# Where the splits of the output weights stand: program order for the gate's and the output's, old states through GpSimd's queue, the samples' last step ranked first

## The chip, the core and the metric

The kernel runs on one core of a Trainium2 chip. The metric is the device time of one execution in microseconds (us), and less is better. Engines are named as in the profile: PE is TensorE (matmuls), DVE is VectorE, ACT is ScalarE, POOL is GpSimd, SP is SyncE, which here only issues transfers. Each engine takes its instructions in the order in which the program stands for it, so an instruction that waits holds up all that stand behind it on its engine.

## The reference

One inference step of a two-layer decoder for 256 prompt positions and 8 sample tokens, handled together as 264 columns. Each layer is half a SwiGLU, a mixer, half a SwiGLU. The mixer of layer 0 is RWKV-7 time mixing, the one of layer 1 a retention.

```python
def step(S, inp):
    r_t, d_t, k_t, v_t, kk_t, a_t = inp
    sa = jnp.einsum('bhvk,bhk->bhv', S, -kk_t)
    S = (S * d_t[:, :, None, :] + sa[..., None] * (kk_t * a_t)[:, :, None, :]
         + v_t[..., None] * k_t[:, :, None, :])
    return S, jnp.einsum('bhvk,bhk->bhv', S, r_t)
...
y = (_head_norm(y, RW_GN_EPS) * lnx_g + lnx_b)
y = y + jnp.sum(r_h * k_h * r_k, axis=-1, keepdims=True) * v_h
out = (y.reshape(B, L, D) * g) @ wo
...
x = x + out
h = _rmsnorm(x, w['ln_ffn2'][i])
x = x + FFN_RES * _swiglu(h, w['ff2_wg'][i], w['ff2_wu'][i], w['ff2_wd'][i])
```

The gate is `g = sigmoid(xg @ g1) @ g2`. The prompt starts from a zero state; each sample has an old state `S` of its own, which is read for `sa` (`S` times the key), for the output row (`S` times decay and receptance) and for the new state that is written out.

## The kernel before

Activations lie transposed: 1024 features as 8 tiles of 128 partitions, 264 columns each (`self.x[:, m, :]`). Weights come as 364 units of 512 KB, each eight 128x128 blocks in the order in which the program uses them. `unit` (line 157) loads a unit into `raw` (three buffers) on SP's queue. `split` (line 163) makes two parts of it in a reduced float format: ACT copies `raw` to `hi`, DVE subtracts `hi` from `raw` to give `lo` (three buffers each). A product of full accuracy is then three matmuls (`mm3`, line 249): `hi` with the high part of the activation, `hi` with its low part, `lo` with its high part. Some weights (key, receptance, value) are not split; their matmuls read `raw` itself (`xv,raw` in the profile).

`rwkv` is written as Python generators: a main one, `stream`, and sides that are woven in (`weave`) by a model of the engines' clocks and by each side's rank. The tile framework then reorders each engine's instructions by a model of its own, except that an instruction handed to `keep_in_program_order` stays behind the one that was written before it on its engine. In `split` this pinning is off (`self.pinned = False`), so the framework may place the ACT copy and the DVE subtraction of a unit wherever its model thinks the unit has landed.

The end of the RWKV part, around the change, in the order of `stream`:

- the value products of the 8 tiles (`xv,raw`); meanwhile the heads, in four groups of two tiles (`heads2`), run many small matmuls on PE with evacuations on ACT and DVE between them. Names of one group: `KQ`, `bT`, `M` (M1), `aT`, `VK`, `z`, `WT`, `G`, `Y`, and `PI`, which POOL makes;
- the gate's second weight, one unit of 8 blocks (`rw_g2`), used at the end of each group;
- the output weight `rw_wo`, 8 units. Output tiles 0 to 3 take four units together, as the groups finish; tiles 4 to 7 take one unit each, 24 matmuls. When tile m is summed, DVE adds it to `x[:, m]`, and `feed(m)` (line 257) prepares the next norm from it: ACT makes `ah` (scaled copy) and the square (`ss` for tile 0, `sq` for the others), DVE makes `al` and adds the square to `ss`.

The samples' old states (`in_wkv`, 2 MB) are read twice here, four loads of 512 KB each time, into `dS` tiles that share three buffers with other tiles: `saved` forms `sa`, `decode_rows` the output rows; both use `states_with` (line 1033), where POOL multiplies a piece by a row and DVE sums it. `decode_rows` is the samples' last step; its rank among the sides is `decode` in the table `TU`, and a lower rank stands earlier.

Of the kernel before, what the change touches and what calls it, by code (L numbers as in the profile page):

```python
# [41 lines left out]
class Step:  # L42
    def __init__(self, ctx, nc, tc, io):
        self.ctx, self.nc, self.tc, self.io = ctx, nc, tc, io
        self.order, self.early = [], {}
        self.done = {}
        self.clock = dict(pe=0.0, dve=0.0, act=0.0, pool=0.0, dma=0.0)
        self.ready = {}
        self.now = self.start = 0.0
        self.table = None  # L50
        self.use(MODEL)
        self.pinned, self.pins = False, ()
        self.late = nc.gpsimd
        e = ctx.enter_context
        self.cp = e(tc.tile_pool(name="cp", bufs=1))
        self.raw_p = e(tc.tile_pool(name="raw", bufs=3))
        self.hi_p = e(tc.tile_pool(name="hi", bufs=3))
        self.lo_p = e(tc.tile_pool(name="lo", bufs=3))
        self.a_p = e(tc.tile_pool(name="a", bufs=18))
        self.w_p = e(tc.tile_pool(name="w", bufs=1))  # L60
        self.ps_p = e(tc.tile_pool(name="ps", bufs=8, space=PSUM))
# [101 lines left out]
    def split(self, raw, first=False):  # L163
        hi = self.hi_p.tile([128, UT, 128], F32R, tag="hi", name="hi")
        lo = self.lo_p.tile([128, UT, 128], F32R, tag="lo", name="lo")
        now, start, self.start = self.now, self.start, 0.0
        pinned, self.pinned = self.pinned, False
        for i, j in FIRST if first else ((0, UT),):
            s = slice(i, j)
            self.act(hi[:, s], raw[:, s])  # L170
            self.tt(lo[:, s], raw[:, s], hi[:, s], ALU.subtract)
        self.now, self.start, self.pinned = now, start, pinned
        if self.model["AHEAD"]:
            for t in (hi, lo):
                self.ready.pop(t.tensor.name, None)
        return hi, lo
# [268 lines left out]
class Rwkv(Step):  # L445
# [18 lines left out]
    def rwkv(self, gain):  # L464
        nc, tc, ps_, late = self.nc, self.tc, self.ps, self.late
# [5 lines left out]
        with ExitStack() as ctx:  # L471
# [68 lines left out]
            def stream():  # L540
                loras = [scaled("wa1", ((0, 64, 1), (64, 128, 4))), scaled("rw_g1", ((0, 128, 5),))]
                acc.extend((ps_(), ps_()) for _ in loras)
                rs = None
                for k0, k1 in ((0, TU["RK"]), (TU["RK"], KT)):
                    for (W0, W2), (Y0, Y2) in zip(loras, acc):
                        for k in range(k0, k1):
                            self.mm3(Y0[:, 0:T], W0[k], xg[k], k == 0, k == KT - 1)
                            self.mm3(Y2[:, 0:T + NS], W2[k], xt[k], k == 0, k == KT - 1)
                            yield
                    if rs is None:  # L550
                        rs = self.rms()

                        for f in range(KT):
                            nc.gpsimd.memset(hz[f][:, 0:1], 0.0)
                            self.stt(hz[f][:, 1:T + 1], self.x[:, f, :], par("ln_mix.0", f), rs)
                            self.tt(xx[f][:, 0:NP], hz[f][:, 0:NP], hz[f][:, 1:NP + 1], ALU.subtract)
                            self.tt(xx[f][:, NP:T], sh[:, f, :], hz[f][:, NP + 1:T + 1], ALU.subtract)
                            mixed("k", 2, f)
                            mark(f"mix{f}")
                            nc.gpsimd.tensor_copy(sho[:, f, :], hz[f][:, NP:T + 1])  # L560
                self.late.dma_start(self.io["sho"], sho)
                wa2.extend(self.wt("wa2", 0, f) for f in range(KT))
                for n, g in (("hidden", hidden(rs)), ("rates", rates()), ("mixr", mixes("r", 0)), ("mixv", mixes("v", 3))):
                    self.beside(TU[n], g)
                if TU["HE"]:
                    heads()
                for g in range(2):
                    kp = [ps_()[:, 0:T] for _ in range(4)]
                    for k in range(KT):
                        yield f"mix{k}"  # L570
                        for j in range(4):
                            prod(kp[j], "k", k, 4 * g + j)
                            yield
                    k_out(g, kp)
                self.beside(TU["inverse"], inverse())
                self.beside(TU["saved"], saved())
                def vs(f):
                    p = ps_()[:, 0:T]
                    for k in range(KT):
                        if f == 0 and "v" not in WHOLE:  # L580
                            yield f"vp{k}"
                        prod(p, "v", k, f)
                        yield
                    values(f, p)

                def rs_(f):
                    p = ps_()[:, 0:T]
                    for k in range(KT):
                        prod(p, "r", k, f)
                        yield  # L590
                    st[f]["rc"] = slot("rc")
                    self.act(st[f]["rc"], p)
                    self.act(dq[:, 4, f, :], p[:, NP:T])
                    mark(f"r{f}")
                    self.beside(TU["prep"], prep(f))

                for i in range(KT + TU["IL"]):
                    if i < KT:
                        yield from rs_(i)
                    if i == KT - 1 and not TU["HE"]:  # L600
                        heads()
                    if i >= TU["IL"]:
                        yield from vs(i - TU["IL"])
                g2.extend(self.wt("rw_g2", 0, f) for f in range(KT))

                po = {}

                def wo(m, k):
                    if k == 0:
                        po[m] = ps_()[:, 0:T]  # L610
                    self.mm3(po[m], self.wt("rw_wo", k, m), go[k], k == 0, k == KT - 1)

                n0, n1 = TU["n0"], TU["n1"]
                for k in range(KT - 1):
                    yield f"go{k}"
                    for m in range(n0):
                        wo(m, k)
                        yield
                for m in range(n0, n1):
                    for k in range(KT - 1):  # L620
                        wo(m, k)
                        yield
                yield f"go{KT - 1}"
                for m in range(KT):
                    for k in range(KT - 1 if m < n1 else 0, KT):
                        wo(m, k)
                        yield
                    self.tt(self.x[:, m, :], po[m], self.x[:, m, :], ALU.add)
                    self.feed(m, gain)

            wa2, g2 = [], []
            A3, AT = (P1.tile([128, 32, 32], F32, name=k) for k in ("A3", "AT"))
# [401 lines left out]
            def states_with(row, out):  # L1034

                def load(i):
                    if i * NV < 64:
                        Sd = by_value(big("dS"))
                        nc.sync.dma_start(Sd, by_value(self.io["wkv"][:, part_of(i)[1]]))
                        return Sd  # L1040

                for i in range(64 // NV):
                    vs = part_of(i)[0]
                    if i == 0:
                        ahead = load(0), load(1)
                        yield 2.5
                    Sd, ahead = ahead[0], (ahead[1], load(i + 2))
                    self.pool_tt(Sd, Sd, row.unsqueeze(1).to_broadcast([128, NV, 64]))
                    yield
                    self.vec("tensor_reduce", Sd, out=out[:, vs], op=ALU.add, axis=AX.X)  # L1050
                    yield
# [76 lines left out]
def by_value(t):  # L1128
    return t.rearrange("p (v k) -> p v k", v=NV)
# [5 lines left out]

NM = 60
NW = 10
TU = dict(PEF=1.0, DVEF=1.0, ACTF=1.5, LP=0.5, LD=0.12, LA=0.15, SLACK=0.2, AHEAD=1, wk='mm', wr='mm', wv='mm', IL=8, pin_stream=0, pin_hidden=1, pin_rates=0, pin_mixes=0, pin_lengths=0, pin_stage=0, pin_inverse=0, pin_prep=1, pin_head=0, pin_saved=0, vp='r7', hv=0, hw=1, hidden=8, rates=7, mixr=1, mixv=5, inverse=0, saved=4, prep=3, head=2, headf=0.01, decode=9, lengths=3, stage=7, by_step=0, HE=0, wait_r=None, wait_v='k0', PW=4, SW=8, RK=3, INVY=8, pre=3.5, n0=3, n1=4)
WHOLE = "krv"
SLOT = 266  # L1140

# [445 lines left out]
```

## Time and profile before

| what | value |
|---|---|
| time, median of 3 runs | 1299.81 us (1299.36 to 1302.5) |
| the profiled execution | 1302.37 us, of which the trace spans 1300.6 us |
| PE busy | 1258.5 us, 97% of the span |
| DVE busy | 866.2 us, 67% |
| ACT busy | 669.0 us, 51% |
| POOL busy | 87.1 us, 7% |
| chain that ended last | 90% PE |

The profiled execution took 2.56 us more than the median of the runs. PE is busy for nearly the whole span, so the time is PE's work plus the stretches in which it stands still or in which its granted clock is at the lower level (1.2 instead of 2.4 GHz, shown as 0.50).

### The profile page before, as it was taken

The numbers are of one execution on the slowest core, as the hardware profiler recorded it, in microseconds if no ns is written. First come the engines' busy times: TensorE is split into PE (matmuls) and PEld (weight loads), VectorE is DVE, ScalarE is ACT, GpSimd is POOL, SyncE is SP. The second block draws the span as 40 slices with busy tenths as digits, with TensorE's granted clock in tenths as the row PEclk, the third lists the DMA queues.
The fourth block names the chain that finished last, engine by engine and source line by source line (L and its number), as shares of the span: only waits on it lengthen the run. The fifth ranks groups of instructions, "written<-read, shape, count | busy, mean of one in ns | idle before, by whom it ended". The sixth has DMA issues, their size and how long they took to land.

```text
span 1300.6 us, 28601 instructions
## 1 busy us (share of the span) xinstructions
PE 1258.5 (97%) x11932; PEld 1187.7 (91%) x11932; DVE 866.2 (67%) x1400; ACT 669.0 (51%) x1162; POOL 87.1 (7%) x177
## 2 busy tenths in 40 slices
PE   9999999998788999999999999999999999999996
PEld 9999998677666899999999999988888799999996
DVE  6766567589355777765666665577878866666654
ACT  6544442652334577764455544455765554544542
POOL 0000001133330000000000000002111100000000
PEclk9999999999979999999999999999999999999998
DMA  7555554232420467665557655669879565555552
GB/s 231 186 185 182 179 162 144 91 124 89 148 84 4 153 200 225 221 198 179 178 178 260 197 184 180 203 237 327 301 286 333 204 196 181 176 184 182 182 178 82
DMA packets 67329, 241.16 MB, mean 185 GB/s; under 512 B 7568, under 2 KB 8976, under 8 KB 67072
## 3 DMA queue, kind: packets, MB, share of 16 engines
q1 hardware_dynamic: 60624, 216.82, 50.8%
q0 software_dynamic: 5968, 21.31, 4.3%
q8 instruction: 93, 1.52, 0.5%
q10 hardware_dynamic: 608, 1.21, 0.3%
q14 instruction: 36, 0.29, 0.1%
HBM read 216.95 MB, written 22.35 MB: 184 GB/s over the span
## 4 chain that ended last, share of the span: by engine, by line
PE 90%; DVE 5%; DMA 2%; ACT 2%; issue 1%; DVEq 0%; SPq 0%; ACTq 0%
PE ps L138 89%; DMA raw<-in_w 2%; DVE tm L105 1%; PE ps L153 1%; DVE V L105 1%; ACT hi L90 1%; DVE lo L105 1%; DMA S<-in_ret 0%; DVE KQ L105 0%; ACT L90 0%; DVE xf L105 0%; DVE A L132 0%; DVE on L120 0%; DVE rs L126 0%; ACT yl L90 0%
## 5 line engine op out<-in xcount | busy, mean ns | idle before, releaser
L90 ACT ACTIVATE hi<-raw 128x1024 fp32r<-128x1024 f32 (+1 forms) x344 | 362.7, 1055 | 447.8 <-PE ps L138 218.9
L105 DVE TENSOR_TENSOR lo<-raw,hi 128x1024 fp32r<-128x1024 f32 (+1 forms) x344 | 418.8, 1218 | 238.5 <-ACT hi L90 237.2
L138 PE MATMUL ps<-ah,hi 128*128 128x264 f32 (+1 forms) x1824 | 522.7, 289 | 0.9 <-ACT ah L90 0.9
L138 PE MATMUL ps<-al,hi 128*128 128x264 f32 (+1 forms) x1824 | 516.9, 285 | 0.0
L138 PE MATMUL ps<-ah,lo 128*128 128x264 f32 (+1 forms) x1824 | 514.5, 285 | 0.0
L138 PEld LDWEIGHTS ps<-ah,hi 128*128 128x128 f32 x1824 | 342.8, 189 | 9.0 <-issue 7.4
L138 PEld LDWEIGHTS ps<-al,hi 128*128 128x128 f32 x1824 | 343.5, 189 | 4.1 <-issue 2.9
L138 PEld LDWEIGHTS ps<-ah,lo 128*128 128x128 f32 x1824 | 342.4, 189 | 0.1
L138 PE MATMUL ps<-hh,hi 128*128 128x264 f32 x832 | 237.1, 285 | 0.0
L138 PE MATMUL ps<-hl,hi 128*128 128x264 f32 x832 | 237.0, 285 | 0.0
L138 PE MATMUL ps<-hh,lo 128*128 128x264 f32 x832 | 236.8, 285 | 0.0
L138 PEld LDWEIGHTS ps<-hl,hi 128*128 128x128 f32 x832 | 156.8, 188 | 0.0
L138 PEld LDWEIGHTS ps<-hh,lo 128*128 128x128 f32 x832 | 156.7, 188 | 0.0
L138 PEld LDWEIGHTS ps<-hh,hi 128*128 128x128 f32 x832 | 156.4, 188 | 0.1
L105 DVE TENSOR_TENSOR h<-s,ps 128x264 f32<-128x264 f32 x88 | 37.1, 428 | 49.0 <-PE ps L138 46.9
L105 DVE TENSOR_TENSOR t<-ps,rs 128x264 f32<-128x264 f32 x88 | 37.2, 431 | 19.2 <-PE ps L138 19.0
L114 DVE SCALAR_TENSOR_TENSOR S<-ps,ks,S 128x512 f32<-128x512 f32 x64 | 45.0, 745 | 5.9 <-PE ps L138 5.9
L90 ACT ACTIVATE S<-S 128x1024 f32<-128x1024 f32 x32 | 33.7, 1055 | 16.9 <-DMA S<-in_ret 16.5
L105 DVE TENSOR_TENSOR hl<-h,hh 128x264 fp32r<-128x264 f32 x88 | 37.0, 428 | 0.3
L90 ACT ACTIVATE hh<-h 128x264 fp32r<-128x264 f32 x88 | 35.3, 408 | 3.6 <-DVE h L105 3.6
L90 ACT ACTIVATE s<-t 128x264 f32<-128x264 f32 x88 | 35.3, 410 | 3.5 <-DVE t L105 3.5
L138 PE MATMUL ps<-part,hi 128*128 128x264 f32 (+1 forms) x176 | 34.5, 309 | 2.3 <-ACT part L90 2.3
(260 smaller groups left out, 1232.9 us busy)
## 6 DMA issues: line engine op xcount, KB each, us to landing
raw<-in_w SPq DMA_DIRECT2D x363, 512.0 KB, 3.5
S<-in_ret SPq DMA_DIRECT2D x32, 512.0 KB, 5.8
out_sret<-S POOLq DMA_DIRECT2D x32, 512.0 KB, 3.7
dS<-in_wkv SPq DMA_DIRECT2D x8, 512.0 KB, 4.0
Sd<-in_wkv SPq DMA_DIRECT2D x4, 512.0 KB, 5.2
out_swkv<-Sd POOLq DMA_DIRECT2D x4, 512.0 KB, 3.8
out_pret<-so POOLq DMA_DIRECT2D x8, 256.0 KB, 2.3
rcst<-in_rcst SPq DMA_DIRECT2D x1, 1100.0 KB, 6.4
```

The lines of the kernel that those rows point to most:

```text
L90: ins = self.nc.scalar.activation(out=out, in_=in_, func=func, scale=scale, **kw)
L105: ins = self.nc.vector.tensor_tensor(out=out, in0=a, in1=b, op=op)
L114: ins = self.nc.vector.scalar_tensor_tensor(out=out, in0=a, scalar=s, in1=b, op0=op0, op1=op1)
L138: ins = self.nc.tensor.matmul(out=out, lhsT=lhsT, rhs=rhs, start=start, stop=stop)
L153: self.nc.tensor.transpose(out, in_, ident)
```

## The change

Three edits. While `stream` is between the last value product and the last output tile, `in_order` is set, and the splits of units first used there keep their place in the program on ACT and DVE: that is the gate's unit and the 8 output units. The `dS` loads are issued by POOL instead of SP. The rank of the samples' last step goes from 9 to 1.

```diff
--- before.py
+++ after.py
@@ -50,6 +50,7 @@
         self.table = None
         self.use(MODEL)
         self.pinned, self.pins = False, ()
+        self.in_order = False
         self.late = nc.gpsimd
         e = ctx.enter_context
         self.cp = e(tc.tile_pool(name="cp", bufs=1))
@@ -164,10 +165,10 @@
         hi = self.hi_p.tile([128, UT, 128], F32R, tag="hi", name="hi")
         lo = self.lo_p.tile([128, UT, 128], F32R, tag="lo", name="lo")
         now, start, self.start = self.now, self.start, 0.0
-        pinned, self.pinned = self.pinned, False
+        pinned, self.pinned = self.pinned, self.in_order
         for i, j in FIRST if first else ((0, UT),):
             s = slice(i, j)
-            self.act(hi[:, s], raw[:, s])
+            self.pin(self.act(hi[:, s], raw[:, s]))
             self.tt(lo[:, s], raw[:, s], hi[:, s], ALU.subtract)
         self.now, self.start, self.pinned = now, start, pinned
         if self.model["AHEAD"]:
@@ -601,6 +602,7 @@
                         heads()
                     if i >= TU["IL"]:
                         yield from vs(i - TU["IL"])
+                self.in_order = True
                 g2.extend(self.wt("rw_g2", 0, f) for f in range(KT))
 
                 po = {}
@@ -627,6 +629,7 @@
                         yield
                     self.tt(self.x[:, m, :], po[m], self.x[:, m, :], ALU.add)
                     self.feed(m, gain)
+                self.in_order = False
 
             wa2, g2 = [], []
             A3, AT = (P1.tile([128, 32, 32], F32, name=k) for k in ("A3", "AT"))
@@ -1036,7 +1039,7 @@
                 def load(i):
                     if i * NV < 64:
                         Sd = by_value(big("dS"))
-                        nc.sync.dma_start(Sd, by_value(self.io["wkv"][:, part_of(i)[1]]))
+                        nc.gpsimd.dma_start(Sd, by_value(self.io["wkv"][:, part_of(i)[1]]))
                         return Sd
 
                 for i in range(64 // NV):
@@ -1135,7 +1138,7 @@
 
 NM = 60
 NW = 10
-TU = dict(PEF=1.0, DVEF=1.0, ACTF=1.5, LP=0.5, LD=0.12, LA=0.15, SLACK=0.2, AHEAD=1, wk='mm', wr='mm', wv='mm', IL=8, pin_stream=0, pin_hidden=1, pin_rates=0, pin_mixes=0, pin_lengths=0, pin_stage=0, pin_inverse=0, pin_prep=1, pin_head=0, pin_saved=0, vp='r7', hv=0, hw=1, hidden=8, rates=7, mixr=1, mixv=5, inverse=0, saved=4, prep=3, head=2, headf=0.01, decode=9, lengths=3, stage=7, by_step=0, HE=0, wait_r=None, wait_v='k0', PW=4, SW=8, RK=3, INVY=8, pre=3.5, n0=3, n1=4)
+TU = dict(PEF=1.0, DVEF=1.0, ACTF=1.5, LP=0.5, LD=0.12, LA=0.15, SLACK=0.2, AHEAD=1, wk='mm', wr='mm', wv='mm', IL=8, pin_stream=0, pin_hidden=1, pin_rates=0, pin_mixes=0, pin_lengths=0, pin_stage=0, pin_inverse=0, pin_prep=1, pin_head=0, pin_saved=0, vp='r7', hv=0, hw=1, hidden=8, rates=7, mixr=1, mixv=5, inverse=0, saved=4, prep=3, head=2, headf=0.01, decode=1, lengths=3, stage=7, by_step=0, HE=0, wait_r=None, wait_v='k0', PW=4, SW=8, RK=3, INVY=8, pre=3.5, n0=3, n1=4)
 WHOLE = "krv"
 SLOT = 266
```

What this does to the order of the instructions, at three places. The first is ACT while the value products end. `hi_4999` is the split of the gate's unit, `hi_5506` and `hi_5619` those of the first two output units, `G`, `Y` and `WT` belong to groups of heads, `vt` is a value tile. Before:

```order
L90 ACTIVATE vt_4336<-ps_4248 128x264
L90 ACTIVATE hi_4999<-raw_4997 128x1024
L90 ACTIVATE G_4410<-ps_4344 128x256
L90 ACTIVATE G_4411<-ps_4345 128x256
L90 ACTIVATE Y_4412<-ps_4344 128x256
L90 ACTIVATE Y_4413<-ps_4345 128x256
L90 ACTIVATE hi_5506<-raw_5504 128x1024
L90 ACTIVATE WT_4457<-ps_4427 128x448
L90 ACTIVATE WT_4458<-ps_4428 128x448
L90 ACTIVATE hi_5619<-raw_5617 128x1024
L90 ACTIVATE vt_4574<-ps_4339 128x264
```

Now:

```order
L91 ACTIVATE vt_4336<-ps_4248 128x264
L91 ACTIVATE G_4410<-ps_4344 128x256
L91 ACTIVATE G_4411<-ps_4345 128x256
L91 ACTIVATE Y_4412<-ps_4344 128x256
L91 ACTIVATE Y_4413<-ps_4345 128x256
L91 ACTIVATE WT_4457<-ps_4427 128x448
L91 ACTIVATE WT_4458<-ps_4428 128x448
L91 ACTIVATE vt_4560<-ps_4339 128x264
```

The three splits have left this place. The gate's stands now behind the last value tile and ahead of the next group's `z`; the first output unit's behind the third `part` (the split of a finished gate-and-norm tile), the second behind the last group's `sd`. DVE's subtractions moved in the same way.

The second place is ACT at output tiles 4 to 7. `hi_5771`, `hi_5810`, `hi_5849`, `hi_5888` are the units of tiles 4, 5, 6, 7; `ah_5761`, `sq_5765` are the feed of tile 3, `ah_5800`, `sq_5804` that of tile 4, `ah_5839`, `sq_5843` of tile 5, `ah_5878`, `sq_5882` of tile 6. Before:

```order
L90 ACTIVATE hi_5771<-raw_5769 128x1024
L90 ACTIVATE part_5648<-yl_5586 128x264
L90 ACTIVATE part_5686<-yl_5592 128x264
L90 ACTIVATE hi_5810<-raw_5808 128x1024
L90 ACTIVATE ah_5729<-x_76,par_77 128x264
L90 ACTIVATE ss_5733<-x_76 128x264
L90 ACTIVATE sq_5743<-x_76 128x264
L90 ACTIVATE hi_5849<-raw_5847 128x1024
L90 ACTIVATE ah_5739<-x_76,par_77 128x264
L90 ACTIVATE hi_5888<-raw_5886 128x1024
```

Now:

```order
L91 ACTIVATE sq_5765<-x_76 128x264
L91 ACTIVATE hi_5771<-raw_5769 128x1024
L91 ACTIVATE ah_5761<-x_76,par_77 128x264
L91 ACTIVATE ah_5800<-x_76,par_77 128x264
L91 ACTIVATE sq_5804<-x_76 128x264
L91 ACTIVATE hi_5810<-raw_5808 128x1024
L91 ACTIVATE ah_5839<-x_76,par_77 128x264
L91 ACTIVATE sq_5843<-x_76 128x264
L91 ACTIVATE hi_5849<-raw_5847 128x1024
L91 ACTIVATE ah_5878<-x_76,par_77 128x264
L91 ACTIVATE sq_5882<-x_76 128x264
L91 ACTIVATE hi_5888<-raw_5886 128x1024
```

Before, the four splits stood far ahead of their own tiles, mixed with the feeds of tiles 0 and 1; now each stands behind the feed of the tile before its own. On PE the order of those products is as it was, now:

```order
L139 MATMUL ps_5768<-part_5686,hi_5771 128x264
L139 MATMUL ps_5768<-part_5687,hi_5771 128x264
L139 MATMUL ps_5768<-part_5686,lo_5772 128x264
L139 MATMUL ps_5807<-part_5467,hi_5810 128x264
L139 MATMUL ps_5807<-part_5468,hi_5810 128x264
L139 MATMUL ps_5807<-part_5467,lo_5811 128x264
```

`ps_5768` is tile 4, `ps_5807` tile 5; nothing stands between the last matmul of one and the first of the next, before and now.

The third place is the queue of the old states. On SP before:

```order
L159 DMA raw<-in_w 128x1024 x7
L1039 DMA dS<-in_wkv 128x1024 x4
L159 DMA raw<-in_w 128x1024
L1039 DMA dS<-in_wkv 128x1024 x2
L159 DMA raw<-in_w 128x1024 x5
L1039 DMA dS<-in_wkv 128x1024
```

On POOL now, where `dS<-dS` are the multiplications and `PI` feeds PE:

```order
L111 TENSOR_TENSOR PI<-cst,PL 128x256 x2
L688 COPY dq<-vt 128x8
L111 TENSOR_TENSOR dS<-dS,w_4571 128x1024 x3
L1042 DMA dS<-in_wkv 128x1024
L111 TENSOR_TENSOR dS<-dS,w_4571 128x1024
L111 TENSOR_TENSOR PI<-cst,PL 128x256 x2
```

SP's queue holds weights only from here on; the eighth load of old states stands on POOL between the multiplications and a `PI`. The new rank moves little: the samples' small matmuls (`cst,dq`) stay within a few rows of where they stood on PE.

## Rows read from the trace of the kernel before

**Rows 1.** Stretches: window, length, busy of each engine, granted clock, DMA share, GB/s.

```profile
360.00:380.00 20.00, 15.05 (x323) 11.32 (x322) 12.78 (x30) 6.71 (x15) 11.46 (x7) 0.70 0.33 114
...
440.00:460.00 20.00, 20.00 (x163) 19.77 (x162) 17.94 (x31) 16.47 (x39) 0.00 (x0) 1.00 0.58 188
```

**Rows 2.** PE in order of time: start, length, instruction, idle before and releaser.

```profile
352.18 0.45 PE L138 MATMUL ps<-G,Ls 64*64 64x64 f32 x8 [0.42 <-ACT G L90]
357.90 1.44 PE L138 MATMUL ps<-PI,be 64*64 64x64 f32 x30 [4.40 <-ACT WT L90]
364.15 0.48 PE L138 MATMUL ps<-cst,dq 64*64 64x64 f32 x4 [3.85 <-ACT vt L90]
365.73 1.25 PE L138 MATMUL ps<-xv,raw 128*128 128x264 f32 x2 [1.10 <-DVE KQ L105]
371.79 0.45 PE L138 MATMUL ps<-G,Ls 64*64 64x64 f32 x8
...
386.28 0.58 PE L138 MATMUL ps<-PI,be 64*64 64x64 f32 x24
```

**Rows 3.** The chain that ended last, 343 to 366 us: start, length, what.

```profile
344.48 5.90 DMA raw<-in_w
...
352.74 3.50 DMA raw<-in_w
...
358.61 4.13 DMA raw<-in_w
```

**Rows 4.** SP's queue, same stretch, in order of time.

```profile
343.56 0.81 SPq L1039 DMA_DIRECT2D dS<-in_wkv  x2
```

**Rows 5.** Stretches around falls of the granted clock; columns as in rows 1.

```profile
354.90:371.40 16.50, 8.55 (x114) 6.21 (x114) 7.43 (x17) 4.58 (x10) 4.89 (x3) 0.50 0.34 112
...
416.60:419.50 2.90, 2.90 (x25) 2.54 (x25) 2.66 (x10) 1.19 (x3) 0.00 (x0) 0.50 0.02 6
429.90:433.20 3.30, 3.30 (x11) 2.94 (x12) 2.05 (x5) 0.16 (x1) 0.00 (x0) 0.50 0.38 148
439.00:446.00 7.00, 7.00 (x58) 6.84 (x57) 6.44 (x12) 5.51 (x11) 0.00 (x0) 1.00 0.37 88
```

**Rows 6.** PE's two longer waits as the output begins, in order of time.

```profile
415.18 0.63 PE L138 MATMUL ps<-part,hi 128*128 128x264 f32 x3 [2.26 <-ACT part L90]
...
429.85 1.62 PE L138 MATMUL ps<-rd,cst 128*128 128x256 f32 x3 [2.45 <-DVE rd L105]
```

**Rows 7.** ACT in order of time, at the output tiles.

```profile
414.70 1.10 ACT L90 ACTIVATE part<-yl 128x264 fp32r<-128x264 f32 x3 [1.95 <-DVE yl L105]
...
438.84 1.06 ACT L90 ACTIVATE hi<-raw 128x1024 fp32r<-128x1024 f32 x1 [4.11 <-PE ps L138]
440.03 0.52 ACT L90 ACTIVATE ah<-x,par 128x264 fp32r<-128x264 f32 x1
440.45 0.41 ACT L90 ACTIVATE ss<-x 128x264 f32<-128x264 f32 x1
440.76 0.41 ACT L90 ACTIVATE sq<-x 128x264 f32<-128x264 f32 x1
```

**Rows 8.** DVE in order of time, at the output tiles.

```profile
442.49 0.43 DVE L105 TENSOR_TENSOR x<-ps,x 128x264 f32<-128x264 f32 x1
...
446.97 1.23 DVE L105 TENSOR_TENSOR lo<-raw,hi 128x1024 fp32r<-128x1024 f32 x1
```

**Rows 9.** POOL in order of time: multiplications, PI, and a store issued by POOL.

```profile
367.48 6.97 POOL L110 TENSOR_TENSOR dS<-dS,w 128x1024 f32<-128x1024 f32 x3 [2.35 <-issue]
...
377.46 1.21 POOL L110 TENSOR_TENSOR PI<-cst,PL 128x256 f32<-128x256 f32 x2
...
473.75 0.54 POOL L1122 DMA_DIRECT2D out_swkv<-Sd  x1 [51.69 <-issue]
```

**Rows 10.** The page's list of transfers: count, size, median us from issue to landing.

```profile
out_swkv<-Sd POOLq DMA_DIRECT2D x4, 512.0 KB, 3.8
```

## The prediction

> **What bounds the kernel now.** I read the stretches first, then PE's own rows, then the chain. PE is 97% busy over the span (the table above); in the feed-forward after the mixer it is busy without a gap at the full clock ([rows 1], 440 to 460). So what the end of the RWKV part gains or loses reaches the end of the kernel undiminished: no slack stands behind it to swallow it. In 360 to 380 PE is busy for only 15.05 of 20 us, and its granted clock is 0.70 ([rows 1]). The reader sees four waits there: 0.42 us for ACT's `G`, 4.40 for `WT`, 3.85 for `vt`, 1.10 for DVE's `KQ` ([rows 2]), 9.77 us together. None of these takes long to make. The chain names what stood ahead of them: three loads of weights, of 5.90, 3.50 and 4.13 us, with the split of each behind it ([rows 3]). ACT's order gives the reason: `hi_4999`, `hi_5506`, `hi_5619` stand ahead of `G`, `WT` and `vt`, and they wait for loads that come late and one after another, since two of the three `raw` buffers still hold value weights. The first load went out at 344.48 behind two loads of old states ([rows 3], [rows 4]).
>
> The clock adds to it. From 354.9 to 371.4 it is 0.50, the level of 1.2 GHz, after PE had stood still; PE is busy for 8.55 us in it ([rows 5]), which at 2.4 GHz would be half, so 4.28 us are lost. **The jam costs 9.77 + 4.28 = 14.05 us.**
>
> **The change, part by part.**
>
> The jam goes. With the three splits out of the way, ACT makes `G` and `Y` right after their sums, `WT` and `vt` as soon as PE has the sums for them, and PE has other matmuls of the same stretch in between. The work of PE at 371.79 ([rows 2]) would come some 14 us earlier. What is late next is the chain of the heads itself, hidden today by the slow clock; I leave 12 us as the lower bound. Taken: -14.0.
>
> The gate's split now stands ahead of the next group's `z`. One ACT copy is 1.06 us ([rows 7]); PE comes to `z` with nothing else to do, so it waits that long: +1.0 (bounds 0.5 and 1.1). DVE's part of this split lies in a DVE pause and costs nothing; were the pause gone, it would be 1.23 us ([rows 8]).
>
> The first output unit. Before, PE began the output at 415.18, when the first `part` was done ([rows 6]); the split had been made long ago. Now `hi_5506` follows three parts, 414.70 + 1.10 + 1.06 = 416.86 ([rows 7]), 1.7 us later, of which 0.4 us are filled by small matmuls of the last group, which moved ahead: +1.3. The second unit waits for the last group's `sd`. This wait takes the place of the 2.45 us at 429.85, where `sd` stood behind another split ([rows 6]); I count some 2.3 us for it (an estimate: two squares of about 0.4 with their handovers, a short `sd`, and `hi` 1.06). Together +1.0, with bounds of -1 (the small matmuls and the last group's earlier end save more) and +2.5 (a further fall of the clock).
>
> **Output tiles 4 to 7 are the part that decides.** In the new order the split of tile m+1 stands on ACT behind `feed(m)`, and `feed(m)` needs the finished sum of tile m. PE has nothing between the last matmul of tile m and the first of tile m+1, and that one reads `hi` of the new unit. So the stations follow each other: DVE's add 0.43 ([rows 8]); `ah`, from its start to the next start 440.45 - 440.03 = 0.42; the square 440.76 - 440.45 = 0.31 by the equal `ss`; `hi` 1.06 ([rows 7]); `lo` 1.23 ([rows 8]); some 0.15 for five handovers: 3.60 us. Two matmuls with `hi` fit in between. 58 matmuls in 7.00 us ([rows 5], last row) are 0.12 each, so PE stands still for 3.60 - 0.24 = 3.4 us. This is so ahead of tiles 5, 6 and 7; ahead of tile 7 four matmuls of the next stage fit in too, so 2.9 there. Ahead of tile 4 the feeds of tiles 0 to 3 come first: three `ah` and four squares, 3 x 0.42 + 4 x 0.31 = 2.5, then 1.06 + 1.23 + 0.15 = 4.9, less 0.24 and 0.1 that the add of tile 0 is ahead: 4.6. Sum 4.6 + 3.4 + 3.4 + 2.9 = 14.3 us of standing still, where now PE is busy for 20.00 of 20 us ([rows 1]). In today's order the work that covers this is the neighbouring tile's products: those splits stand ahead of the feeds.
>
> The clock at these tiles. After each of PE's two waits of 2.26 and 2.45 us ([rows 6]) there is one stretch at 0.50: 2.90 and 3.30 us, full of matmuls ([rows 5]), so 1.45 and 1.65 us lost. The four gaps are longer than these waits. I take 1.5 us for each, 6.0 in all. From below the bound is 0, if the two matmuls in the middle of a gap keep the clock up. From above it is as in the jam, where repeated waits held the clock at 0.50 all through ([rows 5], first row): then all four tiles run at half speed, 4 x 24 matmuls x 0.12 = 11.6 us.
>
> The old states on POOL. SP's queue loses eight issues that stood between weights; the weights come earlier, which is part of the -14.0. POOL gains eight issues of 0.54 us, by its own store of the same size, which lands 3.8 us later ([rows 9], [rows 10]). Behind them on POOL stands `PI`, which PE needs. Today POOL starts the multiplications at 367.48 and PE uses the `PI` of that group at 386.28 ([rows 2], [rows 9]), 18.8 us on. In the new order the row that these need comes some 11.8 us earlier (9.77 of waits and about 2 of half speed lie ahead of it) and PE 13.0, so 18.8 + 11.8 - 13.0 = 17.6 us remain. POOL needs 6.97 for three, 0.54 + 3.8 for the last load, 2.3 for the fourth, 1.21 for `PI`: 14.8. The cover is 2.8 us, so the cost is 0. The upper bound: if the last load took 5.90 us, as the slowest of [rows 3], and three issues were each held for the 1.23 us of the longest DVE instruction in the rows ([rows 8]), `PI` would need 14.8 + 2.1 + 3.7 = 20.6 us, 3.0 too many.
>
> Here the Trainium skill has a rule against the change ("SBUF — State Buffer", section "SBUF: two separate sides"): a transfer issued by GpSimd needs GpSimd to write its descriptors, and a VectorE copy of the fast kind locks GpSimd out until it ends. By the page a transfer of 0.62 us then takes 3.1; as an estimate from that page, one load so held would still be covered and two would cost some 2 us. POOL's own store shows the undisturbed case, and no row here shows the other.
>
> The samples' rank moves a few rows of small matmuls and the weights elsewhere keep their places: 0.
>
> **Sum.** -14.0 + 1.0 + 1.0 + 14.3 + 6.0 + 0 = +8.3 us. Against the profiled execution, 1302.37 us with a span of 1300.6, that gives 1310.7; that execution was 2.56 us above the median of the runs, so the median to compare with is 1299.81 + 8.3 = **1308.1**.
>
> **Rivals.**
>
> *The clock holds in the gaps.* The two matmuls split each gap into about 2.4 and 1.0 us. Against it stand the waits of 2.26 and 2.45 us, both followed by 0.50. Then 8.3 - 6.0 = +2.3, with the first units at their lower bound +0.3: 1300.1 to 1302.1, no change.
>
> *The gaps do not open: faster.* The place is ACT between tiles 4 and 7. If ACT and DVE had the next split done before the sum of a tile ends, as they have today, only the jam's gain is left: -14.0 + 1.0 + 1.0 = -12.0, 1287.8. For it speak ACT's 51% and DVE's 67% of busy time (the table above), and that `raw`, `hi` and `lo` have three buffers each. It decides at a gap, clock included, of (12.0 - 3.9) / 4 = 2.0 us: below that the kernel is faster by over 0.3%. Against it: the printed order, in which the split stands behind the feed, and 3.6 us of stations.
>
> *The clock stays low through all four tiles*, as in the jam, and the second unit's wait makes it fall too: 8.3 + (11.6 - 6.0) + 1.5 = +15.4, 1315.2.
>
> *POOL is late with `PI`.* A load that waits for its buffer or for its descriptors holds POOL, and PE with it, once past the 2.8 us of cover: 8.3 + 3.0 = +11.3, 1311.1. For it, POOL is busy for 11.46 of 20 us in the stretch ([rows 1]); against it, PE's four waits there name ACT and DVE, not POOL ([rows 2]).
>
> **Chances.** 0.3% of the time, 3.9 us, is about what a measurement tells from no change. The forecast (1304 to 1313) 0.60; the clock holds 0.14; the gaps do not open 0.08; the clock stays low 0.10; POOL late 0.08. The forecast, the low clock and POOL are slower: 0.78; same 0.14; faster 0.08. The range 1300 to 1315 leaves out the faster rival and about half of the low clock; the forecast's own range is 1304 to 1313.
>
> **What the new profile would show.** The jam: no wait of PE over 1.2 us between 345 and 365, the clock at 1.00 there, the small matmuls of 371.79 near 358. The gaps: near 425 to 465, four waits of PE for `hi` and `lo`, 2.3 and 1 us in pairs, with a clock of 0.50 in part of the tiles, and ACT's `hi` directly behind `sq`. POOL: eight loads, each under 0.7 us to issue, and no wait of PE for `PI`. The prediction is wrong if these gaps are under 2 us, if the jam's waits stay in another form, or if the feed-forward after it is no longer without gaps.

## The result and the profile after

| | median | runs |
|---|---|---|
| before | 1299.59 us | 4, 1298.55 to 1302.5 |
| changed | 1322.51 us | 4, 1321.66 to 1325.03 |
| ratio | 1.0176 | 95% interval 1.0154 to 1.0198 |

The change costs 22.9 us where 8.3 were forecast. Measured again beside another run of before it cost 19.8. The profiled execution spans 1320.0 us, 19.4 more than that of before.

The first view is the table by stretches, after the change (columns as in [rows 1]: length, then busy time of PE, PEld, DVE, ACT, POOL, then the granted clock, the DMA share and GB/s):

```profile
345.00:360.00 15.00, 14.73 (x481) 11.72 (x474) 6.37 (x22) 4.01 (x12) 6.57 (x7) 1.00 0.34 109
360.00:380.00 20.00, 14.75 (x422) 12.19 (x423) 9.13 (x21) 8.03 (x18) 6.56 (x7) 0.83 0.18 55
...
420.00:440.00 20.00, 15.95 (x97) 15.09 (x98) 12.28 (x24) 6.63 (x14) 0.00 (x0) 0.78 0.34 106
440.00:460.00 20.00, 13.23 (x59) 11.98 (x58) 5.71 (x9) 3.55 (x6) 0.00 (x0) 0.62 0.24 79
```

The same stretch in the kernel before:

```profile
345.00:360.00 15.00, 10.18 (x337) 8.46 (x326) 2.72 (x4) 4.07 (x8) 0.68 (x2) 0.82 0.42 144
```

In 345 to 360 the jam is gone: PE is busy for 14.73 us at 1.00, against 10.18 at 0.82. In 360 to 380 little is won against [rows 1]. In 420 to 460 PE stands still or runs at half speed for much of the time; before, it was busy for 20.00 of 20 us at full clock in 440 to 460 ([rows 1]). PE's waits say who (start, length, what runs, and in brackets the idle time before it and what ended it):

```profile
344.36 0.27 PE L139 MATMUL ps<-VK 64*64 64x64 f32 x2 [2.60 <-DVE rc L106]
...
372.74 2.08 PE L139 MATMUL ps<-rd,cst 128*128 128x256 f32 x4 [3.62 <-DVE rd L106]
...
435.88 0.81 PE L139 MATMUL ps<-part,hi 128*128 128x264 f32 x2 [3.48 <-ACT hi L91]
...
437.14 0.59 PE L139 MATMUL ps<-part,lo 128*128 128x264 f32 x1 [0.45 <-DVE lo L106]
...
444.28 0.51 PE L139 MATMUL ps<-part,hi 128*128 128x264 f32 x2 [2.33 <-ACT hi L91]
...
445.54 0.59 PE L139 MATMUL ps<-part,lo 128*128 128x264 f32 x1 [0.75 <-DVE lo L106]
...
453.08 0.81 PE L139 MATMUL ps<-part,hi 128*128 128x264 f32 x2 [2.33 <-ACT hi L91]
...
454.34 0.59 PE L139 MATMUL ps<-part,lo 128*128 128x264 f32 x1 [0.45 <-DVE lo L106]
...
462.71 0.81 PE L139 MATMUL ps<-part,hi 128*128 128x264 f32 x2 [3.62 <-ACT hi L91]
```

The last seven rows are the gaps ahead of output tiles 4 to 7 that the prediction described. The first two were in no part of it: PE waits for `rc` and for `rd`, both made by DVE. The chain of waits tells why `rd` is late (start, length, what ran):

```profile
355.35 6.98 POOL dS L111 x3
...
362.33 5.43 DMA dS<-in_wkv
...
367.84 2.36 POOL dS L111
...
370.22 1.23 DVE ys L127
...
372.74 10.11 PE ps L139 x293
```

POOL multiplies three pieces of old state, and only then issues the fourth load, because that stands behind them on its queue. The load takes 5.43 us, POOL stands and waits for it, multiplies, DVE sums it (`ys`), and behind that sum stand on DVE the small `sd` and `rd` of the first head group, for which PE waits. In the kernel before, SP issued this load at 371.10, 3.6 us after the first multiplication began at 367.48 ([rows 9]); POOL now issues it 7.0 us after the first begins.

The first pass is late in the same way. Its fourth load went out at 336.15, as the third multiplication ended, and behind the sum `sa` that it holds up stands `rc` on DVE (POOL's row first, then DVE's):

```profile
340.38 2.34 POOL L111 TENSOR_TENSOR dS<-dS,rows 128x1024 f32<-128x1024 f32 x1 [2.09 <-DMA dS<-in_wkv]
...
342.75 1.22 DVE L127 TENSOR_REDUCE sa<-dS 128x16 f32<-128x1024 f32 x1 [5.29 <-POOL dS L111]
343.88 0.76 DVE L106 TENSOR_TENSOR rc<-ps,vt 128x264 f32<-128x264 f32 x2
```

The stretches at half speed, after the change:

```profile
372.70:376.00 3.30, 3.27 (x38) 2.44 (x42) 1.20 (x4) 0.00 (x0) 0.00 (x0) 0.50 0.00 0
437.10:441.50 4.40, 4.36 (x20) 4.37 (x21) 0.38 (x1) 0.00 (x0) 0.00 (x0) 0.52 0.36 119
445.50:450.80 5.30, 5.21 (x22) 4.90 (x22) 0.01 (x1) 0.00 (x0) 0.00 (x0) 0.50 0.33 99
454.30:458.20 3.90, 3.86 (x17) 3.86 (x18) 0.00 (x0) 0.00 (x0) 0.00 (x0) 0.50 0.70 236
463.60:468.70 5.10, 5.04 (x23) 5.04 (x24) 2.59 (x3) 1.91 (x6) 0.00 (x0) 0.50 0.70 190
407.90:412.50 4.60, 4.60 (x31) 4.27 (x31) 4.32 (x12) 1.90 (x4) 0.00 (x0) 0.50 0.22 53
```

The second to the fifth row are the output tiles: (1 - clock) x busy time is 2.1 + 2.6 + 1.9 + 2.5 = 9.1 us lost. The first row follows the wait for `rd` and loses 1.6; the last follows a wait of 2.96 us for DVE's `G` and loses 2.3.

### The profile page after: what moved, and what is told of

The parts are those of the page before. It is cut to its first block, busy times and chain, and to the rows that moved or that the text cites. A ratio compares the mean times of both kernels' runs of the same rounds, so it can differ in the third digit from the quotient of the medians.

```text
span 1320.0 us, 28594 instructions
## 1 busy us (share of the span) xinstructions
PE 1267.3 (96%) x11932; PEld 1194.7 (91%) x11932; DVE 868.1 (66%) x1400; ACT 669.1 (51%) x1162; POOL 89.6 (7%) x185
## 4 chain that ended last, share of the span: by engine, by line
PE 86%; DVE 6%; DMA 3%; ACT 2%; issue 2%; POOL 1%; SPq 0%; DVEq 0%; ACTq 0%; POOLq 0%
PE ps L139 85%; DVE tm L106 1%; POOL dS L111 1%; DMA dS<-in_wkv 1%; DMA S<-in_ret 1%; DVE V L106 1%; PE ps L154 1%; ACT hi L91 1%; DVE lo L106 1%; DMA raw<-in_w 0%; DVE rc L115 0%; DMA Sd<-in_wkv 0%; DVE pp L106 0%; DVE x L106 0%; ACT sq L91 0%
## 5 line engine op out<-in xcount | busy, mean ns | idle before, releaser
L139 PE MATMUL ps<-part,hi 128*128 128x264 f32 (+1 forms) x176 | 41.8, 358 | 13.1 <-ACT hi L91 13.1
L139 PEld LDWEIGHTS ps<-part,hi 128*128 128x128 f32 (+1 forms) x176 | 33.3, 245 | 17.3 <-ACT hi L91 14.2
L91 ACT ACTIVATE ah<-x,par 128x264 fp32r<-128x264 f32 x48 | 24.1, 503 | 26.4 <-DVE x L106 26.4
```

The source lines that it names most:

```text
L91: ins = self.nc.scalar.activation(out=out, in_=in_, func=func, scale=scale, **kw)
L139: ins = self.nc.tensor.matmul(out=out, lhsT=lhsT, rhs=rhs, start=start, stop=stop)
```

## The experiments

The theory after the traces: the jam's gain and the tiles' loss came as reckoned, and on top of them POOL's in-order queue makes `sa` and `ys` late, and with them what stands behind them on DVE. The rivals: POOL's loads cost nothing and the splits cost more than reckoned; POOL's transfers are slow in themselves; the low clock at the tiles comes from something that happened earlier.

Times are medians; each is compared with runs of before on the same chip (1301.1 to 1302.3 us), and the difference is to that.

| run | us | to before | ratio, 95% interval |
|---|---|---|---|
| loads on POOL alone | 1302.24 | -0.1 | 1.0003, 0.9992 to 1.0013 |
| rank alone | 1303.26 | +2.2 | 1.0011, 0.9998 to 1.0024 |
| changed, loads on SP | 1312.24 | +9.9 | 1.0078, 1.0053 to 1.0104 |
| changed, second pass on SP | 1315.82 | +14.7 | 1.0124, 1.0107 to 1.0140 |
| changed, POOL's loads earlier in its queue | 1318.91 | +17.8 | 1.0144, 1.0127 to 1.0161 |
| changed, tiles 4 to 7 free | 1295.92 | -6.4 | 0.9956, 0.9938 to 0.9974 |
| changed, gaps filled | 1318.00 | +15.7 | 1.0116, 1.0095 to 1.0137 |
| loads on SP, tile asked for ahead | 1295.20 | -5.9 | 0.9957, 0.9943 to 0.9971 |
| loads on SP, only the gate in order | 1293.00 | -8.1 | 0.9933, 0.9909 to 0.9957 |
| loads on SP, tiles 4 to 7 free | 1289.77 | -11.3 | 0.9922, 0.9907 to 0.9937 |
| changed, again | 1320.91 | +19.8 | 1.0158, 1.0126 to 1.0189 |
| before, again | 1301.70 | +0.6 | 1.0004, 0.9991 to 1.0018 |

**The loads on POOL, alone.**

```diff
-nc.sync.dma_start(Sd, by_value(self.io["wkv"][:, part_of(i)[1]]))
+nc.gpsimd.dma_start(Sd, by_value(self.io["wkv"][:, part_of(i)[1]]))
```

> The kernel before with one line changed: the eight loads of old states are issued by POOL. Theory A (the loads queue behind POOL's own multiplications, and DVE's reductions, with the work behind them, wait for them): PE loses some 2.6 us near 344, as in the changed kernel, and some 3.6 us ahead of the products with rd, plus 1 to 3 us at half speed: 1306 to 1309 us, with waits of PE for DVE's rc and rd. Theory B (POOL's loads stay hidden, and what the change lost it lost with the splits): 1298 to 1301 us and no such wait. Theory C (with SP freed of eight issues the weights come earlier and the waits for the splits shrink): below 1296 us.

No change in time against before, as theory B had it, but not for its reason: two effects cancel. PE's waits:

```profile
345.81 0.27 PE L138 MATMUL ps<-VK 64*64 64x64 f32 x2 [2.03 <-DVE rc L105]
...
361.10 0.48 PE L138 MATMUL ps<-cst,dq 64*64 64x64 f32 x4 [4.00 <-ACT vt L90]
...
380.48 2.06 PE L138 MATMUL ps<-rd,cst 128*128 128x256 f32 x4 [3.28 <-DVE rd L105]
```

Theory A's waits are there, 2.03 us for `rc` and 3.28 for `rd`. Of the four waits of the jam ([rows 2]) the two for `G` and `WT`, 0.42 and 4.40 us, are gone, because SP gets to the weights earlier (its next unit goes out at 334.33, before at 338.84), which is theory C. So alone the edit costs nothing; with the jam removed otherwise, only its cost is left. How much that is depends on the rest of the order: with tiles 4 to 7 free it is 4.9 us (-6.4 against -11.3 in the table), with them in order 10 to 13.

**The changed kernel with the loads on SP again** (the line above, back):

> The changed kernel with the loads of old states back on SP; splits in program order and the samples' rank stay. Theory A: the waits of PE for rc (2.6 us) and rd (3.6 us) and the half speed behind them go: 1313 to 1317 us; the four gaps at the output tiles stay as they are. Theory B: 1320 to 1324 us, no change. Rival to both: with the loads on SP the weights wait behind them again, some wait for a split comes back, and the time is above 1324 us.

10 to 13 us come back, more than theory A's 6 to 9. The wait for `rc` is gone, with a new one of 1.34 us for `vt` in that region, and 1.04 is left of the one for `rd`:

```profile
350.50 0.45 PE L139 MATMUL ps<-G,Ls 64*64 64x64 f32 x8 [1.34 <-ACT vt L91]
...
367.32 1.13 PE L139 MATMUL ps<-rd,cst 128*128 128x256 f32 x4 [1.04 <-DVE rd L106]
```

The products with `rd` start at 367.32, 13.7 us earlier than the 381.00 of before and 5.4 earlier than in the changed kernel. POOL's two rows for the second pass:

```profile
354.49 6.99 POOL L111 TENSOR_TENSOR dS<-dS,w 128x1024 f32<-128x1024 f32 x3 [4.65 <-issue]
...
362.41 2.36 POOL L111 TENSOR_TENSOR dS<-dS,w 128x1024 f32<-128x1024 f32 x1 [0.93 <-DMA dS<-in_wkv]
```

SP issues the fourth load at 358.47, beside the multiplications, and POOL waits 0.93 us for it, not 4.92.

**One pass each.** Only the second pass on SP:

```diff
+(nc.gpsimd if out is sa else nc.sync).dma_start(Sd, ...)
```

> The changed kernel with the four loads of the second pass (the one that makes ys) back on SP; those of the first pass (sa) stay on POOL. Before stands at 1302 us on the chip of the runs so far, the changed kernel 22.9 us above it, and with both passes on SP 9.9 above it. Theory A (each pass costs its own wait: rc near 344 the first, rd near 370 the second): the wait for rd falls to some 1 us as with both on SP, the one for rc stays at 1.4 to 4 us; two thirds of the 13 us come back, 1314 to 1318 us. Rival (the second pass is late only because the first made everything late): the wait for rd stays above 2.5 us, 1321 to 1326 us.

The wait for `rd` falls to 0.88, that for `rc` stays (3.61), and the time is in theory A's range. By these medians the first pass costs 14.7 - 9.9 = 4.8 us, the second the other 5 to 8.

**Queue order or slow transfers?** The third and fourth load of the second pass are placed behind the first and second multiplication on POOL; the other engines keep their order.

```diff
+if out is ys and i > 1:
+    self.tc.keep_in_program_order(ins)
...
-Sd, ahead = ahead[0], (ahead[1], load(i + 2))
+Sd = ahead[0]
 self.pool_tt(Sd, Sd, row.unsqueeze(1).to_broadcast([128, NV, 64]))
+ahead = ahead[1], load(i + 2)
```

> The changed kernel with the third and fourth load of the second pass pinned on POOL's queue behind the first and second multiplication instead of behind all three; every other engine keeps its order. Theory A (the load is late because it stands behind POOL's own multiplications): the fourth multiplication ends 12.3 us after the first began (three loads and products in turn, each load 0.59 + 3.6, each product 2.3), not 14.9 as in the changed kernel; PE's wait for rd falls from 1.8 to 5.6 to 0 to 1.5 us, and the time is 14 to 19 us above before (both passes on POOL: 20 to 23, second pass on SP: 14.7). Rival (POOL's own transfers are slow, whatever stands ahead of them): the loads take over 5 us to land, the wait for rd stays above 1.8 us, 19 to 24 us above before.

POOL's queue now:

```profile
356.56 2.40 POOL L111 TENSOR_TENSOR dS<-dS,w 128x1024 f32<-128x1024 f32 x1 [3.18 <-DVE w L106]
358.91 0.59 POOL L1042 DMA_DIRECT2D dS<-in_wkv  x1
359.52 2.37 POOL L111 TENSOR_TENSOR dS<-dS,w 128x1024 f32<-128x1024 f32 x1
361.83 0.59 POOL L1042 DMA_DIRECT2D dS<-in_wkv  x1
363.45 2.35 POOL L111 TENSOR_TENSOR dS<-dS,w 128x1024 f32<-128x1024 f32 x1 [1.03 <-DMA dS<-in_wkv]
366.34 2.36 POOL L111 TENSOR_TENSOR dS<-dS,w 128x1024 f32<-128x1024 f32 x1 [0.53 <-DMA dS<-in_wkv]
```

From the first multiplication to the end of the fourth it takes 12.1 us (forecast 12.3; 14.9 in the changed kernel), and the time is in theory A's range. But the runs, 1315.70 to 1321.00 us, overlap those of the changed kernel measured again (1316.22 to 1326.15), so the gain is shown by the trace and not by the time. The wait of PE is not as theory A had it:

```profile
371.24 2.07 PE L139 MATMUL ps<-rd,cst 128*128 128x256 f32 x4 [3.43 <-DVE rd L106]
```

`rd` is ready 14.6 us after the multiplications begin, not 17.3, but PE came to it earlier too. So the order of the queue is part of the delay, and not all: these two loads land only 4.5 us after their issue begins, in the middle of a chain in which each product needs its load. That is less than the rival's 5 us, so neither theory holds whole.

**Tiles 4 to 7 free.** `in_order` ends ahead of the last loop:

```diff
 yield f"go{KT - 1}"
+self.in_order = False
 for m in range(KT):
```

> The changed kernel with the program order of splits ended ahead of output tiles 4 to 7; the splits of the gate and of the first four units stay in order. Theory A (gaps of 13.4 us at these tiles, and 11.0 us lost because PE then runs at half speed): both go, 24.4 us: 1296 to 1301 us, PE without a wait over 1 us in these tiles and a clock of 1.00. Rival (the clock is low there for what happened earlier, not for the gaps): only the 13.4 us go, 1308 to 1311 us, clock of about 0.6 in the tiles.

Theory A, the time just under its range: no wait of PE over 0.4 us in the tiles, a clock of 1.00 from 420 to 460, and 26 to 29 us less than the changed kernel (forecast 24.4).

**The gaps filled.** Behind tiles 3 to 6:

```diff
+pd, w = ps_()[:, 0:T], go[0][0]
+for i in range(22):
+    self.mm(pd, w[:, 0:128], w, i == 0, i == 21, behind=True)
```

> The changed kernel with 22 added matmuls of 128x264 behind each of output tiles 3 to 6, on operands that are long there, into a PSUM tile that nobody reads: at 0.12 us each 2.6 us, about as long as a gap. The order of splits stays. Theory A (the clock falls because PE stands still): the tiles run at full speed, 11.0 us come back, the filling costs at most 1 us: 1310 to 1314 us, clock 1.00 in the tiles. Rival (the clock is low for another cause): the tiles stay at half speed, the fillers last 4.8 us each and stick out of the gaps by some 1.5: 1326 to 1330 us.

The clock is 1.00 from 440 to 460, and the fillers take 2.8 us each, with a short wait for `lo` behind them:

```profile
443.29 2.81 PE L139 MATMUL ps<-part 128*128 128x264 f32 x22
...
447.05 0.39 PE L139 MATMUL ps<-part,lo 128*128 128x264 f32 x1 [0.71 <-DVE lo L106]
```

```profile
440.00:460.00 20.00, 17.71 (x139) 17.08 (x140) 7.04 (x13) 6.47 (x11) 0.00 (x0) 1.00 0.33 106
```

So the low clock at the tiles came of the gaps there, and not of something earlier. The time is 4 to 7 us below the changed kernel, not the expected 8 to 12: the fillers with the waits beside them are longer than the gaps, and in this profile the waits for `rc` and `rd` were 3.95 and 5.63 us, longer than in the others.

**Where the split stands, or that it is fixed?** Loads on SP, order kept, but the weights of the next tile asked for one tile ahead:

```diff
+def split_ahead(m):
+    for k in range(KT if m < KT else 0):
+        ahead[k, m] = self.wt("rw_wo", k, m)
...
+split_ahead(n1)
 for m in range(KT):
+    if m >= n1:
+        split_ahead(m + 1)
```

> The changed kernel with all eight loads back on SP, and, splits still in program order, the weights of output tile m+1 asked for ahead of the products of tile m, so that its split stands ahead of that tile's feed. Theory A (what decides at the tiles is where the split stands, not that its place is fixed): no wait over 1 us in the tiles, clock 1.00, 9.9 - 24 to 27 us against before: 1285 to 1289 us. Rival (a fixed order makes some other wait there, a split ahead of its weights or a feed behind it): 1293 to 1303 us with new waits of PE in the tiles.

The time is in the rival's range. Of the 21.2 us that the tiles cost with the loads on SP, 15.8 come back (9.9 + 5.9), so most of the cost lies in where the split stands. But two waits of over 1 us stay, and behind the second the clock was 0.55 for 3.8 us:

```profile
428.22 0.51 PE L139 MATMUL ps<-part,hi 128*128 128x264 f32 x2 [1.17 <-ACT hi L91]
...
439.20 0.57 PE L139 MATMUL ps<-part,lo 128*128 128x264 f32 x1 [2.02 <-DVE lo L106]
```

The split of tile 5 now stands behind the feeds of tiles 0 to 2, so it is still late by what they take. The second wait is ahead of tile 7: there DVE waited 2.46 us for a piece of old state, `Sd`, that stood ahead of `lo` on its queue. The placement by the framework was better than either fixed order.

**Only the gate in order**, loads on SP (`in_order = False` right behind the gate's unit):

> The changed kernel with the loads on SP, and only the gate's split in program order; all splits of the output are placed by the planner, which puts the first two output units behind the gate's split and ahead of the next group's z. Against before at 1301 us. Theory A (a split whose weights are late holds back what stands behind it on ACT): z and what follows wait for two loads, PE stands still for 4 to 9 us near 370 to 380, and half or more of the 11.3 us that the version with the first four units in order won is lost: 1294 to 1302 us. Rival (the gate's split alone made the jam): 1287 to 1291 us, no wait over 1.5 us near 370 to 380.

Neither range. The three splits ran in one piece of 2.98 us without waiting for weights, so theory A's wait is only 1.25 us. Before's waits for `part` and `rd` ([rows 6]) are back:

```profile
372.72 0.90 PE L139 MATMUL ps<-z,X 64*64 64x64 f32 x30 [1.25 <-ACT z L91]
...
404.82 0.64 PE L139 MATMUL ps<-part,hi 128*128 128x264 f32 x3 [2.26 <-ACT part L91]
...
419.52 1.61 PE L139 MATMUL ps<-rd,cst 128*128 128x256 f32 x4 [2.46 <-DVE rd L106]
```

These two, 4.72 us, don't explain why it is slower than the next version: there waits of 2.96, 0.51 and 1.38 us, 4.85 in all, stand in the same place. Of the 4.1 us between the two profiles 2.5 lie ahead of the products with `rd` (369.73 against 367.22), where PE already stood still for 1.80 us at 327.60 (0.21 there in the other), ahead of anything that the order of these splits touches. The runs overlap too: one of the four took 1287.55 us. So most of the gain comes with the gate's split alone, and what the first four units add isn't told from none.

**Loads on SP and tiles 4 to 7 free**, so that the gate and the first four output units alone are in order:

> The changed kernel with the loads back on SP and the program order of splits ended ahead of output tiles 4 to 7: of the change only the order of the gate's and the first four output units and the samples' rank are left. Theory A (the terms add: the jam's 14 us come back whole, nothing is lost at the tiles): 1286 to 1290 us. Rival (with the heads' end some 14 us earlier the output runs into its weights, and part is lost there): 1292 to 1298 us, with waits of PE for raw or hi in the output.

```profile
345.00:360.00 15.00, 13.58 (x395) 10.67 (x394) 7.29 (x24) 4.05 (x12) 5.88 (x4) 1.00 0.37 121
360.00:380.00 20.00, 18.09 (x588) 14.69 (x590) 10.69 (x23) 11.16 (x28) 5.01 (x5) 1.00 0.23 75
420.00:440.00 20.00, 20.00 (x166) 20.00 (x165) 17.87 (x30) 14.42 (x31) 0.00 (x0) 1.00 0.71 227
```

Theory A. This is the fastest version, 11.3 us below before: full clock without the jam's waits, and no gap in the tiles.

**The rank alone, and both kernels again:**

> The kernel before with the samples' last step ranked first and nothing else. Both theories: within 2 us of before, 1300 to 1304 us. If it is more than 4 us away, the rank is a term that the sums left out.

> The changed kernel once more, on the chip of these runs. 20 to 23 us above before; PE's waits for rc and rd between 1.4 and 4.0 and between 3.3 and 5.6 us, as the runs with POOL's loads had them.

> The kernel before once more, for a second profile. Both theories: the same waits near 345 to 365 (0.4, 4.4, 3.9 and 1.1 us) and at 415 and 430; time within 0.3% of before.

The rank's difference isn't told from none. The changed kernel came out 19.8 us above before, just under the range, with runs from 1316 to 1326 us; its waits for `rc` and `rd` were 1.69 and 1.84 in this profile against 2.60 and 3.62 in the first, and that for `rd` is under what was expected. The kernel before showed its waits again: 1.02, 4.43, 4.02, 1.10.

## Why the prediction missed, step by step

**The jam, -14.0: right; the gate's split and the first units, +2.0: right in sum only.** With the loads on SP the products with `rd` moved by 13.7 us. Jam, gate and first units together are the version with the loads on SP and free tiles: -11.3 against the forecast's -12.0, which the prediction gave as the rival "the gaps do not open". What it said the gate's split would cost (1.0) doesn't show as a wait of PE, and the first units' waits are others than it named: 2.96 us for DVE's `G` was in no part of it.

**The gaps, +14.3, and the clock, +6.0: right in sum.** 1312.24 - 1289.77, each against before, is 9.9 + 11.3 = 21.2 us for the four tiles; forecast 20.3. By the waits above the gaps are 3.93 + 3.08 + 2.78 + 3.62 = 13.4 us (14.0 with the loads on SP), the stations as reckoned:

```profile
442.45 0.52 ACT L91 ACTIVATE ah<-x,par 128x264 fp32r<-128x264 f32 x1 [6.22 <-DVE x L106]
442.88 0.41 ACT L91 ACTIVATE sq<-x 128x264 f32<-128x264 f32 x1
443.19 1.04 ACT L91 ACTIVATE hi<-raw 128x1024 fp32r<-128x1024 f32 x1
```

```profile
441.99 0.43 DVE L106 TENSOR_TENSOR x<-ps,x 128x264 f32<-128x264 f32 x1 [4.50 <-PE ps L139]
...
444.26 1.23 DVE L106 TENSOR_TENSOR lo<-raw,hi 128x1024 fp32r<-128x1024 f32 x1 [0.42 <-ACT hi L91]
...
459.28 1.23 DVE L106 TENSOR_TENSOR Sd<-Sd,rows 128x1024 f32<-128x1024 f32 x1 [5.00 <-DMA Sd<-in_wkv]
```

From the start of the add at 441.99 to the first product with `lo` at 445.54 it is 3.55 us (forecast 3.60). Ahead of tile 4 the gap is shorter than the 4.6 said, and ahead of tile 7 longer than the 2.9: DVE had to wait for a piece of old state, `Sd`, and summed it ahead of the add (last row). The clock's 6.0 was too low: it measured 9.1 (8.9 with the loads on SP). I had taken one stretch of 3 us for each gap from [rows 5], and the stretches were 3.9 to 5.3 us long, about halfway to the rival "the clock stays low" (11.6).

**The old states on POOL, +0: wrong, and this is the miss.** It is 19.8 to 22.9 less 9.9, so 10 to 13 us, outside the bounds of 0 to 3.0. The sum is then -11.3 + 21.2 + 10 to 13 = 20 to 23; it closes because each term is a difference of the same runs, and it holds for this order of the edits alone (with the tiles free the loads cost 4.9). The step failed in three ways. It asked who waits for POOL's next product, `PI`, and found 2.8 us of cover; PE indeed never waits for `PI`. It didn't ask what stands on DVE behind the sums `sa` and `ys` that wait for POOL: `rc` in one pass, `rd` in the other. And it priced only the second pass. The rival "POOL is late with `PI`" named the right engine and the wrong path, and stopped at 3.0 us.

By the traces the products with `rd` start 5.2 to 5.4 us later than with the loads on SP (372.74 and 372.49 against 367.32). From 320 to 500 us PE stands still for 30.2 and 31.0 us in the changed kernel's two profiles and for 26.1 with the loads on SP, so some 4 to 5 us of the loss are standing still. The clock's part differs from run to run: in windows of 0.5 us over the same stretch, (1 - clock) x busy time is 17.2 and 10.7 us in the two profiles, 12.3 with the loads on SP. Why the medians are as far apart as 10 to 13 us stays open in part.

**The page's rule.** The Trainium skill ("SBUF — State Buffer", section "SBUF: two separate sides") has POOL's transfers held while VectorE runs a copy of the fast kind, by a factor of five in its example. In the trace they land in 4.2 us (median) against 4.0 on SP in the kernel before, and POOL issues one in 0.53 to 0.61 us, so no such factor shows here. But at these issues VectorE ran sums and other operations and no such copy, so no run here shows the page's own case. The page spoke against the change for another reason than the one that cost the time.

**The signs.** No wait over 1.2 us between 345 and 365 and a clock of 1.00 until 360: seen. Gaps in pairs (only one wait, for `hi`, ahead of tile 7), `hi` directly behind the square: seen. Loads under 0.7 us to issue, no wait for `PI`: seen. None of the signs looked at `rc` or `rd`: the wait for `rc` ends at 344.36, just ahead of the signs' window, and that for `rd` at 372.74, behind it.

## What to carry to other kernels

When work moves to another in-order queue, follow two queues: what stands behind it on the new engine, and what stands behind its consumers on theirs. An edit that costs nothing alone may have been paid for by a jam that another edit removes: price each edit in the order of the finished kernel, not in that of the kernel before. A fixed order helps where the framework places a copy too early for its data, and hurts where it had hidden that copy well: here the same pinning was worth 11 us ahead of the tiles, 8 of them with the gate's split alone, and cost 21 inside them, of which 16 came back when the fixed place was one tile earlier.

## What the runs showed of the hardware

The same wait does not always have the same price. PE's wait of 2.96 us for `G` ahead of the output stands in all nine profiles with the first units in order. In seven of them a stretch at 0.50 begins within 2 us of its end; in two (the changed kernel again, and the second pass on SP) none does. In the changed kernel's first profile it is followed by 0.50 from 407.9 to 412.5 (last row of the half-speed stretches above); in its second by the full clock:

```profile
406.00:412.00 6.00, 5.67 (x62) 5.12 (x63) 5.59 (x18) 2.16 (x5) 0.18 (x1) 1.00 0.27 89
```

So a clock term taken from one profile has an uncertainty of some 2 us for each wait of this length. In the changed kernel's repeat the spread goes with the clock: its four runs took 1316.22, 1320.59, 1321.22 and 1326.15 us at mean granted clocks of 0.986, 0.982, 0.979 and 0.976. As an estimate from these numbers, 0.010 of some 1320 us is 13 us, enough for the 10 us between them. In the first four runs (1321.66 to 1325.03 us at 0.977 to 0.982) the clock doesn't order the times, so it is not shown to be the only cause.

At the tiles, PE's standing still is what went ahead of the low clock: 22 added matmuls in each gap, 2.8 us whose result nobody needs, left the clock at 1.00 from 440 to 460, where it was 0.62 without them.
